# A scan on VectorE in place of matmul sums in stick breaking, and the first projection as filling work

## The chip, the cores and the metric

One core of a Trainium2 chip. The time is that of one execution on the device, in microseconds (us); lower is better. The engines are TensorE (PE: matmuls; PEld is its weight load), VectorE (DVE), ScalarE (ACT), GpSimd (POOL) and SyncE (SP, which issues DMAs). Each runs its own instruction queue in the order in which the program was written out, and waits on semaphores for the others.

## The reference

Two layers of a transformer: 512 tokens, width 1024. Each layer mixes two attentions and then runs a convolutional feed-forward part. The first attention (sparse, 8 heads) gives `o_nsa`; the second is stick breaking:

```python
z = jnp.einsum('bqhd,bkhd->bhqk', q[:, q0:q1], k[:, :q1]) * scale
log_1m = jnp.where(strict, -jax.nn.softplus(z), 0.0)
later = lax.cumsum(log_1m, axis=3, reverse=True) - log_1m
w = jnp.where(strict, jnp.exp(jax.nn.log_sigmoid(z) + later), 0.0)
...
y = g_a * (o_nsa @ w_proj_nsa) + g_b * (o_sb @ w_proj_sb)
return y @ w_out
```

`strict` keeps the keys before the query. Since log_sigmoid(z) is z - softplus(z), the weight of a key is exp(z minus the sum of softplus over this key and all later ones before the query). `g_a` and `g_b` are sigmoids of two more projections of the input.

## The kernel before

Activations lie transposed, with features on partitions and the 512 tokens along the row. All matmuls run in fp32r; a number is split in a high part (a cast on ScalarE, line 105 for weights) and a low part (a subtraction, line 106), and a product takes three matmuls (high x high, low x high, high x low). A full tile over 1024 features is 24 matmuls of 512 columns, a projection tile over 512 features is 12.

The text below calls the stage from the first score matmul of stick breaking to the first matmul of the output projection (`bk<-yh`) "the stage". In it PE has two kinds of work. The first is the eight heads (`Head`). For a head, `scores` writes 1280 columns of PSUM (`Z`, two buffers): keys on partitions, queries along the row, four blocks of 512, 384, 256 and 128 columns. `soft1` to `soft4` build softplus from |z| with Exp and Ln on ScalarE, take max(z, 0) to it on VectorE (line 1066), clear the diagonal blocks on GpSimd (`diag_keep`, line 1034) and split it (lines 1071, 1072). `sums` adds the suffix sums into the same PSUM by matmuls against two constant matrices, `negl` (a triangle of -1) and `nones` (all -1): 10 matmuls for the high part, 10 for the low. `weights1` and `weights2` take Exp, clear the diagonal again and split (lines 1089, 1090); `out` multiplies with the values into `pv`, and the result is added to `o_s`.

The second kind is filling work, tiles that write the one PSUM bank `f`: queries and keys of head pairs 2 and 3 (`sb_pair`; each evacuated by line 781) and the eight tiles of the second gate `gb` (`gate`, line 802). After them comes the projection of the first attention's output `o_n` with gate `ga` (`projection(ga, ...)`, eight tiles in six banks `bk`, evacuated by line 1147), then that of `o_s` with `gb`.

The sparse attention ends just ahead of the stage: transposes `tp` are copied by ScalarE into `pt` and multiplied into `pv`; in between PE puts the values' tiles (`sb_values`).

The order on each engine is not written by hand: a scheduler writes it out at build time from priorities and its own idea of durations. `tc.high_priority(offset=2000)` lifts heads 4 to 7 over the filling tiles. At run time nothing is reordered, so an instruction waits behind everything ahead of it in its queue.

Of the kernel before, what the change touches and what calls it, by code (L numbers as in the profile page):

```python
# [158 lines left out]
def run_kernel(ctx, tc, xT, pos, inv, vec, pew, cw1, w_m, w_vn, w_pr, w_o, w_u, w_d, xmid, rot, out):  # L159
# [116 lines left out]
    negl = cp.tile([128, 128], FR, name="negl")  # L276
# [7 lines left out]
    def constants():  # L284
        with pool("scr") as sp:
            scr = sp.tile([128, 128], F, name="scr")
            scr2 = sp.tile([128, 2, 128], F, name="scr2")
            nc.gpsimd.memset(ident, 1.0)
            nc.gpsimd.affine_select(out=ident, in_=ident, compare_op=OP.is_equal, fill=0.0, base=0,
                                    pattern=[[-1, 128]], channel_multiplier=1)  # L290

            nc.gpsimd.memset(scr, -1.0)
            nc.gpsimd.affine_select(out=scr, in_=scr, compare_op=OP.is_ge, fill=0.0, base=0,
                                    pattern=[[-1, 128]], channel_multiplier=1)
# [12 lines left out]
            nc.vector.tensor_copy(identb, ident)  # L307
            nc.vector.tensor_copy(negl, scr)
            nc.vector.tensor_copy(cbias, scr2)

    def rope_tables(rt, res, wait):
# [212 lines left out]
    for l in range(DEPTH):  # L524
# [8 lines left out]
        def slot(k, name, dt=F):  # L533
            return rp.tile([128, SLOT], dt, name=nm(name), tag=k)
# [291 lines left out]

        def split_o(src, c0, c1):

            hi, lo = slot(c0, "oh", FR), slot(c1, "ol", FR)
            s2 = src.rearrange("p k t -> p (k t)")  # L830
            for k in range(4):
# [188 lines left out]

        with temps(3) as sw, pool("pz", space=PSUM) as pz:

            c0 = [0, 512, 1024, 896]
            wd = [512, 384, 256, 128]

            def blk(t, j, q0=0):

                o = c0[j] + (max(q0, j) - j) * 128
                return t[:, o:c0[j] + wd[j]]

            def diag_keep(t):
                for j in range(4):
                    d = t[:, c0[j]:c0[j] + 128]
                    nc.gpsimd.affine_select(out=d, in_=d, compare_op=OP.is_gt, fill=0.0, base=0,  # L1034
                                            pattern=[[1, 128]], channel_multiplier=-1)

            class Head:
                def __init__(self, h):
# [5 lines left out]
                def scores(self):  # L1044
# [4 lines left out]
                    ks = lambda j: slice(j * 128, j * 128 + 128)  # L1049

                    for j in range(4):
                        mm(blk(Z, j), kk[:, e, ks(j)], qh[:, e, j * 128:], j != 3, False)
                    for j in range(4):
                        mm(blk(Z, j), kk[rr, e, ks(j)], qlo[rr, j * 128:], False, True)

                def soft1(self):
                    t = self.t = self.tile("sbt", "sbt")
                    nc.scalar.activation(t, self.Z[:, :1280], AF.Abs)  # L1058
# [5 lines left out]
                def soft3(self):  # L1064
                    t = self.t
                    nc.vector.scalar_tensor_tensor(t, self.Z[:, :1280], 0.0, t, op0=OP.max, op1=OP.add)
                    diag_keep(t)

                def soft4(self):
                    self.hi, self.lo = self.tile("sph", "sph", FR), self.tile("spl", "spl", FR)  # L1070
                    nc.vector.tensor_copy(self.hi, self.t)
                    nc.vector.tensor_sub(self.lo, self.t, self.hi.bitcast(F))

                def sums(self):
                    Z = self.Z
                    for part in (self.hi, self.lo):
                        for j in range(4):
# [4 lines left out]
                def weights1(self):  # L1082
                    w_ = self.w = self.tile("sbw", "sbw")
                    act(w_, self.Z[:, :1280], AF.Exp)

                def weights2(self):
                    diag_keep(self.w)
# [15 lines left out]
            def run_heads(hs):  # L1103
                for h in hs:
# [253 lines left out]
```

## Time and profile before

| what | value |
|---|---|
| median of three runs | 1656.79 us (1656.38 to 1658.58) |
| the profiled execution, its own time | 1653.88 us |
| its span, first to last instruction | 1652.2 us |
| PE, VectorE, ScalarE, GpSimd busy | 97%, 68%, 50%, 13% |
| mean granted clock of PE | 0.989 of full |

Busy shares are over the whole span; where an engine waits is seen in the lists of waits and in the timeline, which gives each instruction's start, length and the idle time before it with the instruction that ended it.

### The profile page before, as it was taken

How to read it: one execution, taken by the hardware profiler on the slowest of the kernel's cores; microseconds unless marked ns; L12 is line 12 of the kernel's file. 1: busy time of each engine (PE TensorE's matmuls, PEld its weight loads, DVE VectorE, ACT ScalarE, POOL GpSimd, SP SyncE). 2: the span in 40 equal slices, each digit the busy share in tenths (PEclk: the TensorE clock that was granted, in tenths of full speed). 3: DMA queues.
4: the chain of work that ended last, by engine and by line, in shares of the span. 5: the costliest groups of instructions: out<-in, count | busy, mean ns of one | idle time of the engine just before them, and what ended most of it. 6: DMA issues, size and time to landing. Idle time of an engine off the chain costs nothing.

```text
span 1652.2 us, 23212 instructions
## 1 busy us (share of the span) xinstructions
PE 1609.0 (97%) x8970; PEld 1393.2 (84%) x8970; DVE 1118.2 (68%) x1659; ACT 825.3 (50%) x1338; POOL 211.1 (13%) x252
## 2 busy tenths in 40 slices
PE   9899999999999999999999999999999999999997
PEld 9878887888998888888998788878889988888896
DVE  8775676767578777733677666677676687776235
ACT  6555565654555444423555455575536454444233
POOL 0034442120000000000000453322200000000000
PEclk9989999999999999999999999999999999999999
DMA  6521112114412233333664211112153132322344
GB/s 228 152 77 52 39 39 64 52 64 141 132 61 88 91 102 91 97 93 107 195 204 129 71 44 47 39 64 64 52 180 114 39 99 93 102 91 95 98 128 141
DMA packets 53501, 159.42 MB, mean 96 GB/s; under 512 B 6544, under 2 KB 12176, under 8 KB 53392
## 3 DMA queue, kind: packets, MB, share of 16 engines
q1 hardware_dynamic: 51088, 152.00, 29.0%
q0 software_dynamic: 1296, 4.72, 0.8%
q8 instruction: 70, 1.15, 0.3%
q10 hardware_dynamic: 1008, 1.23, 0.3%
q14 instruction: 39, 0.32, 0.1%
HBM read 144.30 MB, written 4.72 MB: 90 GB/s over the span
## 4 chain that ended last, share of the span: by engine, by line
PE 82%; DVE 8%; ACT 5%; issue 2%; DMA 2%; POOL 1%; SPq 1%; ACTq 0%; DVEq 0%; POOLq 0%
PE bk L382 56%; PE f L382 15%; PE pv L382 3%; PE Z L382 3%; PE S L382 2%; PE tp L935 2%; POOL sbt L1034 1%; DVE wlo L106 1%; DVE st L906 1%; DMA rs<-rf 1%; DMA x<-in_xT 1%; ACT whi L105 0%; ACT sbt L226 0%; ACT sbt L1058 0%; ACT sbw L226 0%
## 5 line engine op out<-in xcount | busy, mean ns | idle before, releaser
L105 ACT CAST whi<-wraw 128x1024 fp32r<-128x1024 f32 (+2 forms) x235 | 241.2, 1027 | 342.7 <-PE bk L382 254.3
L106 DVE TENSOR_TENSOR wlo<-wraw,whi 128x1024 fp32r<-128x1024 f32 (+2 forms) x209 | 248.8, 1191 | 184.1 <-ACT whi L105 181.4
L382 PE MATMUL bk<-h_hi,whi 128*128 128x512 f32 (+1 forms) x768 | 286.5, 374 | 2.1 <-ACT f_t L1260 1.7
L382 PE MATMUL bk<-h_hi,wlo 128*128 128x512 f32 (+1 forms) x768 | 286.4, 374 | 0.0
L382 PE MATMUL bk<-h_lo,whi 128*128 128x512 f32 (+1 forms) x768 | 286.2, 373 | 0.0
L382 PE MATMUL f<-h_hi,whi 128*128 128x512 f32 x448 | 184.4, 412 | 11.7 <-DVE gate L802 9.2
L382 PE MATMUL f<-h_lo,whi 128*128 128x512 f32 x448 | 179.1, 400 | 0.0
L382 PE MATMUL f<-h_hi,wlo 128*128 128x512 f32 x448 | 178.6, 399 | 0.0
L382 PEld LDWEIGHTS bk<-h_hi,whi 128*128 128x128 f32 x768 | 145.6, 190 | 27.7 <-ACT f_t L1260 1.9
L382 PEld LDWEIGHTS bk<-h_hi,wlo 128*128 128x128 f32 x768 | 145.5, 190 | 25.4 <-DVE wlo L106 0.4
L382 PEld LDWEIGHTS bk<-h_lo,whi 128*128 128x128 f32 x768 | 145.6, 190 | 24.8
L382 PE MATMUL bk<-ah,wlo 128*128 128x256 f32 (+1 forms) x484 | 161.7, 334 | 2.4 <-DVE wlo L106 2.4
L382 PE MATMUL bk<-ah,whi 128*128 128x256 f32 (+1 forms) x484 | 160.4, 331 | 0.0
L382 PE MATMUL bk<-al,whi 128*128 128x256 f32 (+1 forms) x484 | 160.2, 331 | 0.0
L382 PEld LDWEIGHTS f<-h_hi,whi 128*128 128x128 f32 x448 | 86.4, 193 | 30.6 <-DVE gate L802 10.0
L382 PEld LDWEIGHTS bk<-ah,wlo 128*128 128x128 f32 x484 | 91.8, 190 | 12.5 <-DVE wlo L106 3.4
L1228 DVE TENSOR_TENSOR cu<-bk,r 128x512 f32<-128x512 f32 x88 | 60.2, 687 | 61.2 <-PE bk L382 60.9
L382 PEld LDWEIGHTS f<-h_hi,wlo 128*128 128x128 f32 x448 | 85.9, 192 | 18.5
L382 PEld LDWEIGHTS f<-h_lo,whi 128*128 128x128 f32 x448 | 86.5, 193 | 15.5
L382 PEld LDWEIGHTS bk<-ah,whi 128*128 128x128 f32 x484 | 91.9, 190 | 8.7
L382 PEld LDWEIGHTS bk<-al,whi 128*128 128x128 f32 x484 | 91.9, 190 | 8.7
L382 PE MATMUL bk<-h_hi,wh 128*128 128x256 f32 x512 | 96.0, 285 | 0.0
(241 smaller groups left out, 3174.3 us busy)
## 6 DMA issues: line engine op xcount, KB each, us to landing
wraw<-in_w_u SPq DMA_DIRECT2D x88, 512.0 KB, 3.5
wraw<-in_w_m SPq DMA_DIRECT2D x72, 512.0 KB, 3.3
wraw<-in_w_d SPq DMA_DIRECT2D x44, 512.0 KB, 3.5
wraw<-in_w_d SPq DMA_DIRECT2D x22, 384.0 KB, 3.1
wraw<-in_w_pr SPq DMA_DIRECT2D x16, 512.0 KB, 3.6
wraw<-in_w_o SPq DMA_DIRECT2D x16, 512.0 KB, 3.5
rs<-rf SPq DMA_DIRECT2D x56, 64.0 KB, 2.8
wraw<-in_cw SPq DMA_DIRECT2D x4, 512.0 KB, 4.6
```

What stands on the lines that cost most here:

```text
L105: self.nc.scalar.copy(hi[:, c], raw[:, c])
L106: eng.tensor_sub(lo[:, c], raw[:, c], hi.bitcast(F)[:, c])
L382: last_mm[0] = nc.tensor.matmul(o, a, b, start=first, stop=last, skip_group_check=True)
L906: nc.vector.tensor_reduce(self.st[:, 0:2], self.S[:, :self.n].rearrange("p (j b k) -> p b j k", j=self.i + 1, b=2), axis=AX.XY, op=OP.max, ...
L935: nc.tensor.transpose(tp[:, b * 128:(b + 1) * 128], self.P[:, (c + b) * 128:(c + b + 1) * 128], ident)
L1034: nc.gpsimd.affine_select(out=d, in_=d, compare_op=OP.is_gt, fill=0.0, base=0, pattern=[[1, 128]], channel_multiplier=-1)
L1228: nc.vector.tensor_mul(u, b, r2)
```

## The change

Stick breaking now has queries on partitions and keys along the row, so that the suffix sum runs along a row. `scores` adds a bias block `sbias` (0 below the diagonal, -1e30 from it on) with four bf16 matmuls. `soft1` also takes Relu(z) into `r`; `sums` is a reversed `tensor_tensor_scan` on VectorE in four pieces (512, 384, 256 and 128 columns; line 1075) that adds both parts of softplus up, and a subtraction from `Z` (line 1077). The weights are then transposed on PE, ten 128 x 128 blocks a head in fp32 (line 1085), into the PSUM of `Z`, and split from there: high part on ScalarE (line 1088, `wh`), low part on VectorE (line 1089). GpSimd's masks and the 20 matmuls of sums go. `Z` stays in use until line 1089.

The projection of `o_n` moves ahead of heads 4 to 7 in program order and writes the bank `f`; its low part goes to the buffer of `h_lo`. The two sigmoids of `ga` move ahead of heads 0 to 3.

```diff
+                    for i in (3, 2, 1, 0):
+                        mm(rows(Z, i), qh[:, e, qt(i)], kk[:, e, :(i + 1) * 128], i != 0, False)
+                    for i in (3, 2, 1, 0):
+                        mm(rows(Z, i)[:, i * 128:], identb, sbias, False, False)
+                    for i in (3, 2, 1, 0):
+                        mm(rows(Z, i), qlo[rr, qt(i)], kk[rr, e, :(i + 1) * 128], False, True)
...
+                    r = self.r = self.tile("sbr", "sbr", bufs=2)
+                    nc.scalar.activation(r, z, AF.Relu)
...
-                def sums(self):
-                    Z = self.Z
-                    for part in (self.hi, self.lo):
-                        for j in range(4):
-                            mm(blk(Z, j), negl, blk(part, j), False, False)
-                            for j2 in range(j + 1, 4):
-                                mm(blk(Z, j, j2), nones, blk(part, j2), False, part is self.lo and j2 == 3)
...
+                def sums(self):
+
+                    t, r = self.t, self.r
+                    for i in (3, 2, 1, 0):
+                        nc.vector.tensor_tensor_scan(rows(r, i, True), rows(t, i, True), rows(r, i, True), 0.0,
+                                                     op0=OP.add, op1=OP.add)
+                    nc.vector.tensor_sub(t, self.Z[:, :1280], r)
+
+                def weights(self):
                     t = self.t
...
+                    act(t, t, AF.Exp)
+                    wT = self.Z
+                    for j in range(4):
+                        for i in range(j, 4):
+                            nc.tensor.transpose(blk(wT, j)[:, (i - j) * 128:(i - j + 1) * 128],
+                                                rows(t, i)[:, j * 128:(j + 1) * 128], ident)
                     self.whi, self.wlo = self.tile("wh", "wh", FR), self.tile("wl", "wl", FR)
...
+                    nc.scalar.copy(self.whi, wT[:, :1280])
+                    nc.vector.tensor_sub(self.wlo, wT[:, :1280], self.whi.bitcast(F))
...
+            for i in range(2):
+                act(ga[i], ga[i], AF.Sigmoid)
             run_heads(range(4))
...
             gate(gb, 0, "k1")
             gate(gb, 1, "sa")
+
+            n_hi, n_lo = split_o(o_n, "sb", None)
+            for m in range(8):
+                if m % 2 == 0:
+                    wt = W.get()
+                b = fbank("f")
+                drain(gemm(b, wt, n_hi, n_lo, range(4), woff=4 * (m % 2), ahead=2 if m % 2 else 1))
+                with tc.high_priority():
+                    nc.vector.tensor_mul(at(ga, m), b, at(ga, m))
             with tc.high_priority(offset=2000):
                 run_heads(range(4, 8))
...
-                for m in projection(ga, n_hi, n_lo):
-                    pass
```

How the written order changes is shown at three places of the first layer. The first is ScalarE's queue at the end of the sparse attention: `P_315` is the last softmax, `gate_340` and `gate_345` are `ga`, `pt` the copies of transposed weights. Before:

```order
L226 ACTIVATE P_315_2090,st_314_2083<-S_309_2046,st_314_2083 128x4x128 x2
L968 COPY pvl_311_2069<-pv_310_2052 64x256
L944 CAST pt_303_2030<-tp_312_2073 128x4x128
L944 CAST pt_305_2032<-tp_313_2078 128x4x128
L105 CAST whi30_2747<-wraw30_2631 128x1024
```

And of the change:

```order
L226 ACTIVATE P_315_2092,st_314_2085<-S_309_2048,st_314_2085 128x4x128 x2
L233 ACT_TABLE_LOAD
L226 ACTIVATE gate_340_2344<-gate_340_2344 128x2048
L226 ACTIVATE gate_345_2473<-gate_345_2473 128x2048
L233 ACT_TABLE_LOAD
L969 COPY pvl_311_2071<-pv_310_2054 64x256
L945 CAST pt_303_2032<-tp_312_2075 128x4x128
L945 CAST pt_305_2034<-tp_313_2080 128x4x128
L105 CAST whi30_2749<-wraw30_2633 128x1024
```

Two table loads and both sigmoids of `ga` now stand ahead of the copies of `tp_312` and `tp_313`.

The second is PE's queue where head 0 (`Z_367`) comes back after its scores; `f_407` before and `f_403` now are filling tiles. Before:

```order
L382 MATMUL f_407_3068<-h_hi_99,wlo30_2748 128x512
L382 MATMUL Z_367_2771<-sph_369_2789,negl_94 128x512
L382 MATMUL Z_367_2771<-sph_369_2789,nones_93 128x384
L382 MATMUL Z_367_2771<-sph_369_2789,nones_93 128x256
L382 MATMUL Z_367_2771<-sph_369_2789,nones_93 128x128
L382 MATMUL Z_367_2771<-sph_369_2789,negl_94 128x384
```

And of the change:

```order
L382 MATMUL f_403_3061<-h_hi_99,whi31_3008 128x512
L382 MATMUL f_403_3061<-h_lo_100,whi31_3008 128x512
L382 MATMUL f_403_3061<-h_hi_99,wlo31_3009 128x512
L1085 MATMUL Z_367_2776<-ident_91,sbt_368_2789 128x128 x10
L382 MATMUL f_405_3100<-h_hi_99,whi32_3047 128x512
```

Where the sums of the first half stood, the ten transposes of the finished weights stand now; ahead of them come two filling tiles, behind them `f_405`.

The third is VectorE's queue for heads 0 and 1 (`sbt_368` and `sbr_369`, then `sbt_377` before, `sbt_375` and `sbr_376` now); `sbz` is the evacuation of a filling tile. Before:

```order
L1066 SCALAR_TENSOR_TENSOR sbt_368_2780<-Z_367_2771,sbt_368_2780 128x1280
L789 TENSOR_TENSOR qlo_404_3028<-sbz_406_3060,sbst_403_3027 64x512 x2
L1071 CAST sph_369_2789<-sbt_368_2780 128x1280
L781 SCALAR_TENSOR_TENSOR sbz_408_3099<-f_407_3068,r2_90 128x512
L1072 TENSOR_TENSOR spl_370_2790<-sbt_368_2780,sph_369_2789 128x1280
L106 TENSOR_TENSOR wlo32_3094<-wraw32_2711,whi32_3093 128x1024
```

And of the change (the scan appears under its opcode's name, SCALAR_TENSOR_TENSOR, at line 1075):

```order
L1075 SCALAR_TENSOR_TENSOR sbr_369_2793<-sbt_368_2789,sbr_369_2793 128x512
L1075 SCALAR_TENSOR_TENSOR sbr_369_2793<-sbt_368_2789,sbr_369_2793 128x384
L1075 SCALAR_TENSOR_TENSOR sbr_369_2793<-sbt_368_2789,sbr_369_2793 128x256
L1075 SCALAR_TENSOR_TENSOR sbr_369_2793<-sbt_368_2789,sbr_369_2793 128x128
L789 TENSOR_TENSOR sbst_395_2981<-sbz_400_3053,sbst_395_2981 64x512 x2
L1077 TENSOR_TENSOR sbt_368_2789<-Z_367_2776,sbr_369_2793 128x1280
L1075 SCALAR_TENSOR_TENSOR sbr_376_2844<-sbt_375_2841,sbr_376_2844 128x512
L1075 SCALAR_TENSOR_TENSOR sbr_376_2844<-sbt_375_2841,sbr_376_2844 128x384
L1075 SCALAR_TENSOR_TENSOR sbr_376_2844<-sbt_375_2841,sbr_376_2844 128x256
L1075 SCALAR_TENSOR_TENSOR sbr_376_2844<-sbt_375_2841,sbr_376_2844 128x128
L781 SCALAR_TENSOR_TENSOR sbz_404_3092<-f_403_3061,r2_90 128x512
```

The evacuation of `f_403`, which `f_405` needs, stands behind the whole scan of head 1.

## Rows read from the trace of the kernel before

**Rows 1.** The page, part 1: busy time of each engine.

```profile
PE 1609.0 (97%) x8970; PEld 1393.2 (84%) x8970; DVE 1118.2 (68%) x1659; ACT 825.3 (50%) x1338; POOL 211.1 (13%) x252
```

**Rows 2.** PE's waits, 258 to 400 us: total, times, longest (us).

```profile
PE f L382 <- DVE sbz L781: 0.8, 1, 0.8
PE Z L382 <- ACT sbw L226: 0.6, 1, 0.6
PE pv L382 <- DVE wl L1090: 0.3, 1, 0.3
PE Z L382 <- DVE sph L1071: 0.2, 1, 0.2
PE bk L382 <- ACT whi L105: 0.2, 1, 0.2
```

**Rows 3.** Timeline of PE: first score matmul, and first of the output projection.

```profile
258.33 0.80 PE L382 MATMUL Z<-sbst 128*128 128x512 f32 x4
...
411.66 0.40 PE L382 MATMUL bk<-yh,whi 128*128 128x512 f32 x1
```

**Rows 4.** Timeline of PE: a filling tile, a half of head 0's sums, what follows.

```profile
270.56 0.45 PE L382 MATMUL f<-h_hi,whi 128*128 128x512 f32 x1
...
275.43 0.39 PE L382 MATMUL Z<-spl,negl 128*128 128x512 f32 x1
...
276.74 0.45 PE L382 MATMUL f<-h_hi,whi 128*128 128x512 f32 x1
```

**Rows 5.** Timeline of PE, sparse attention: a bf16 bias matmul, six transposes.

```profile
221.90 0.28 PE L382 MATMUL S<-cbias,identb 128*128 128x256 bf16 x1
222.02 0.84 PE L935 MATMUL tp<-ident,P 128*128 128x128 f32 x6
```

**Rows 6.** Groups by line and shape: busy us, mean ns of one, idle before.

```profile
L105 ACT CAST whi<-wraw 128x1024 fp32r<-128x1024 f32 x211 | 221.7, 1051 | 294.9 <-PE bk L382 206.6 <-PE f L382 52.7 <-issue 30.7
...
L226 ACT ACTIVATE sbt<-sbt 128x1280 f32<-128x1280 f32 x32 | 40.8, 1274 | 0.7
...
L1066 DVE SCALAR_TENSOR_TENSOR sbt<-Z,sbt 128x1280 f32<-128x1280 f32 x16 | 23.8, 1489 | 8.5 <-ACT sbt L226 8.5
...
L1058 ACT ACTIVATE sbt<-Z 128x1280 f32<-128x1280 f32 x16 | 19.9, 1243 | 23.3 <-DVE spl L1072 20.0 <-PE Z L382 3.3
...
L906 DVE TENSOR_REDUCE st<-S 128x2 f32<-128x1024 f32 x16 | 19.5, 1216 | 3.2 <-PE S L382 3.2
...
L1071 DVE CAST sph<-sbt 128x1280 fp32r<-128x1280 f32 x16 | 13.7, 855 | 7.8 <-POOL sbt L1034 5.3 <-PE f L382 2.4
...
L906 DVE TENSOR_REDUCE st<-S 128x2 f32<-128x256 f32 x16 | 6.3, 415 | 1.0 <-PE S L382 1.0
```

**Rows 7.** Timeline of PE: last matmul of a filling tile, first of the next.

```profile
261.98 0.39 PE L382 MATMUL f<-h_hi,wlo 128*128 128x512 f32 x1
263.15 0.50 PE L382 MATMUL f<-h_hi,whi 128*128 128x512 f32 x1 [0.78 <-DVE sbz L781]
```

**Rows 8.** Timeline, ScalarE and PE: the sparse attention's end, and the sigmoids.

```profile
241.44 0.37 ACT L968 COPY pvl<-pv 64x256 f32<-64x256 f32 x1
...
244.95 0.59 ACT L944 CAST pt<-tp 128x512 fp32r<-128x512 f32 x1 [3.14 <-PE tp L935]
...
246.35 0.28 PE L382 MATMUL pv<-pt,vN 128*128 128x256 f32 x1
...
367.32 1.28 ACT L233 ACT_TABLE_LOAD   x1
368.62 7.33 ACT L226 ACTIVATE gate<-gate 128x2048 f32<-128x2048 f32 x4
```

**Rows 9.** Windows: length, busy of each engine, granted clock, DMA share, GB/s.

```profile
116.00:120.00 4.00, 0.17 (x2) 0.00 (x0) 3.75 (x4) 1.08 (x2) 3.10 (x2) 0.80 0.00 0
120.00:124.00 4.00, 3.81 (x9) 3.04 (x10) 2.29 (x7) 1.02 (x4) 1.04 (x1) 0.50 0.37 131
124.00:128.00 4.00, 4.00 (x16) 3.20 (x16) 0.00 (x0) 0.00 (x0) 0.00 (x0) 0.85 0.00 0
```

More of the change, by code (lines that the diff above doesn't have):

```diff
@@ L275, in run_kernel @@
     nones = cp.tile([128, 128], FR, name="nones")
-    negl = cp.tile([128, 128], FR, name="negl")
+    sbias = cp.tile([128, 128], BF, name="sbias")
     cbias = cp.tile([128, 2, 128], BF, name="cbias")
@@ L290, in constants @@
                                     pattern=[[-1, 128]], channel_multiplier=1)
-            nc.gpsimd.memset(scr, -1.0)
-            nc.gpsimd.affine_select(out=scr, in_=scr, compare_op=OP.is_ge, fill=0.0, base=0,
+            nc.gpsimd.memset(scr, 0.0)
+            nc.gpsimd.affine_select(out=scr, in_=scr, compare_op=OP.is_gt, fill=NEG, base=0,
                                     pattern=[[-1, 128]], channel_multiplier=1)
@@ L307, in constants @@
             nc.vector.tensor_copy(identb, ident)
-            nc.vector.tensor_copy(negl, scr)
+            nc.vector.tensor_copy(sbias, scr)
             nc.vector.tensor_copy(cbias, scr2)
@@ L827, in split_o @@
         def split_o(src, c0, c1):
-            hi, lo = slot(c0, "oh", FR), slot(c1, "ol", FR)
             s2 = src.rearrange("p k t -> p (k t)")
+            hi = slot(c0, "oh", FR)
+            lo = slot(c1, "ol", FR) if c1 else h_lo.rearrange("p k t -> p (k t)")
             for k in range(4):
@@ L1021, in run_kernel, with rows, blk @@
         with temps(3) as sw, pool("pz", space=PSUM) as pz:
-            c0 = [0, 512, 1024, 896]
             wd = [512, 384, 256, 128]
[L1026 to L1031, printed above, removed]
-                for j in range(4):
-                    d = t[:, c0[j]:c0[j] + 128]
-                    nc.gpsimd.affine_select(out=d, in_=d, compare_op=OP.is_gt, fill=0.0, base=0,
-                                            pattern=[[1, 128]], channel_multiplier=-1)
+            cq = [896, 1024, 512, 0]
+            ck = [0, 512, 1024, 896]
+            def rows(t, i, rev=False):
+                s_ = t[:, cq[i]:cq[i] + wd[3 - i]]
+                return s_[:, ::-1] if rev else s_
+            def blk(t, j):
+                return t[:, ck[j]:ck[j] + wd[j]]
             class Head:
@@ L1048, in scores @@
                     rr = slice(e * 64, e * 64 + 64)
[L1049 to L1054, printed above, removed]
+                    qt = lambda i: slice(i * 128, i * 128 + 128)
+                    for i in (3, 2, 1, 0):
+                        mm(rows(Z, i), qh[:, e, qt(i)], kk[:, e, :(i + 1) * 128], i != 0, False)
@@ L1056, in soft1 @@
+                    for i in (3, 2, 1, 0):
+                        mm(rows(Z, i)[:, i * 128:], identb, sbias, False, False)
+                    for i in (3, 2, 1, 0):
+                        mm(rows(Z, i), qlo[rr, qt(i)], kk[rr, e, :(i + 1) * 128], False, True)
                 def soft1(self):
-                    t = self.t = self.tile("sbt", "sbt")
-                    nc.scalar.activation(t, self.Z[:, :1280], AF.Abs)
+                    t = self.t = self.tile("sbt", "sbt", bufs=2)
+                    z = self.Z[:, :1280]
@@ L1059, in soft1 @@
+                    nc.scalar.activation(t, z, AF.Abs)
                     act(t, t, AF.Exp, scale=-1.0)
+                    r = self.r = self.tile("sbr", "sbr", bufs=2)
+                    nc.scalar.activation(r, z, AF.Relu)
                 def soft2(self):
                     act(self.t, self.t, AF.Ln, bias=1.0)
-                def soft3(self):
-                    t = self.t
-                    nc.vector.scalar_tensor_tensor(t, self.Z[:, :1280], 0.0, t, op0=OP.max, op1=OP.add)
-                    diag_keep(t)
@@ L1069, in soft4 @@
[L1069 to L1072, printed above, removed]
-                def sums(self):
-                    Z = self.Z
-                    for part in (self.hi, self.lo):
-                        for j in range(4):
-                            mm(blk(Z, j), negl, blk(part, j), False, False)
-                            for j2 in range(j + 1, 4):
-                                mm(blk(Z, j, j2), nones, blk(part, j2), False, part is self.lo and j2 == 3)
@@ L1082, in weights1 @@
[L1082 to L1087, printed above, removed]
+                def sums(self):
[4 more added lines that the diff above has]
+                    nc.vector.tensor_sub(t, self.Z[:, :1280], r)
@@ L1090, in weights2 @@
-                    nc.vector.tensor_sub(self.wlo, self.w, self.whi.bitcast(F))
+                    nc.scalar.copy(self.whi, wT[:, :1280])
+                    nc.vector.tensor_sub(self.wlo, wT[:, :1280], self.whi.bitcast(F))
                 def out(self):
@@ L1130, in run_kernel @@
             m_last = []
-            n_hi, n_lo = split_o(o_n, "sb", "vn")
             s_hi, s_lo = split_o(o_s, "q0", "k0")
-            for g_ in (ga, gb):
-                for i in range(2):
-                    act(g_[i], g_[i], AF.Sigmoid)
+            for i in range(2):
+                act(gb[i], gb[i], AF.Sigmoid)
             with pool("py", space=PSUM) as py:
```

6 lines of the change are left out of this document (1 added, 5 removed).

## The prediction

> **What bounds the kernel now.** First the page: TensorE (PE) is busy 97% of the span [rows 1], and its mean clock is 0.989 of full (the table above). So a microsecond of matmul work is worth about a microsecond wherever PE does not wait, and a wait costs as much. The list of waits over the first layer's stick breaking (258 to 400 us) shows what PE waits for there: five waits, 2.1 us in all [rows 2]. The other engines keep up because PE's queue always has a filling matmul ready. Whatever the change does, it shows on PE, as less work or as more waiting. I measure a layer from the first score matmul of head 0 to the first matmul of the output projection: 258.33 to 411.66, or 153.3 us [rows 3].
>
> I call the heads h0 to h7 and the filling tiles K2, Q3, K3 (`sb_pair`), G0 to G7 (`gate`) and P0 to P7 (first attention's projection).
>
> **PE work removed and added.** One half of a head's sums (10 matmuls) takes 275.43 to 276.74, 1.31 us [rows 4]; two halves, eight heads: 21.0 us per layer gone. Added are ten fp32 transposes a head. Six in a row take 0.84 us with the last one's own 0.27 in it, so 0.114 each [rows 5]: 1.14 a head, 9.1 per layer. Also added are four bf16 bias matmuls of 128 columns. The 256-column one is followed 0.12 us later by the next instruction [rows 5], so 0.06 each; with their weight loads I take 0.3 a head, 2.4 per layer. Scores, outputs and the eight P tiles keep their matmuls. Net: 21.0 - 9.1 - 2.4 = **9.5 us per layer less PE work.** GpSimd loses its masks and gives nothing back, since PE never waited for it there [rows 2].
>
> **What a head now costs the other engines.** Prices are from [rows 6]. ScalarE: Abs 1.24, Exp 1.27, Ln 1.27 and last Exp stay (the last now from SBUF, 1.27); Relu and the copy `wh` are new and are priced like the Abs, which reads the same 1280 columns of PSUM: 1.24 each. VectorE loses a max-add, two casts and two subtractions (1.49 + 0.86 + 1.49 + 0.86 + 1.49; the subtractions have the max-add's shape) and gets the scan and two subtractions.
>
> The trace holds no scan. Reductions of 256 and 1024 columns take 0.415 and 1.216 us: 1.04 ns a column and 0.15 fixed. Below, then: four pieces, 1280 columns, one pass: 1.9 us. Above: two separate passes, 3.9. Each element needs two adds, and the second must be finished before the next element's first can start; I take two passes with the fixed part paid once, 2 x 1.33 + 4 x 0.15 = 3.3. In a queue a VectorE row starts about 0.08 before the one ahead ends, so the walk below uses 3.1 (and 1.7 and 3.6 for the bounds).
>
> The rows show only one-pass operations at 1.04 ns a column. [...]
>
> So VectorE's total hardly moves (6.2 before, 6.3 now), but ScalarE carries 2.5 us more, and the chain of one head is longer: score, Abs, (Relu), Exp, Ln, scan, subtraction, Exp, before its transposes.
>
> **The walk.** I follow the written order of the engines, from PE's first score matmul of h0 = 0. The 21 filling matmuls from 270.56 to 275.43 take 0.232 each [rows 4], so a full tile (24) 5.5 and a P tile (12) 2.8; scores, two passes of 0.8 [rows 3] and the bias, 1.95. The bank `f` is one buffer: when two filling tiles stand next to each other, PE waits for the evacuation, 0.94 us from the last start to the next [rows 7]; with VectorE free I charge 1.0.
>
> - h0's and h1's scores end at 1.95 and 3.9. ScalarE does Abs and Relu of both (2.2 to 7.3), both Exps (to 9.9), a weight cast (10.9), Ln of h0 at 12.2. The scan runs 12.25 to 15.35, then two `L789` pieces (16.6), the subtraction (18.1), Exp (19.4).
> - PE: K2 to 9.45, wait 1.0, Q3 to 16.0. Now it needs h0's transposes: **wait 3.5**, to 19.5. They end at 20.5, and K3 needs Q3's evacuation, which stands on VectorE behind h1's scan (18.1 to 21.2) and ends at 21.85: **wait 1.4**.
> - h2, h3: G1 waits 0.5 (evacuation behind h2's scan), G2 1.0, G3 1.5 (behind h3's scan and subtraction), G4 1.0.
> - h5: Ln at 82.1, scan 85.25, cast, subtraction 87.8, Exp 89.15; PE is at its transposes at 87.1: **2.1**.
> - P0 0.45, P1 1.05 (bank again; before, the projection had six banks).
> - h7: Ln 109, scan 113, `wlo` 114.1, subtraction 115.5, Exp 116.8; PE is there at 112.95: **3.95**.
> - The two sigmoids of `gb` with their table loads come before h7's `wh` on ScalarE (to 123.2); P4 1.0, h7's output 0.55, P5 1.4, P6 1.0.
>
> Together **21.5 us of waiting** where 2.1 were [rows 2]; the output projection starts at 159.6. The same walk with the scan at 1.7 gives 13.5 and 151.6: 5.9 us per layer for each us of scan.
>
> **Ahead of it.** The `ga` sigmoids now stand on ScalarE before `pvl_311` and the copies of `tp_312`, which ran at 241.44 and 244.95. Two table loads of 1.28 and two sigmoids of 1.9 are 6.3 us [rows 8]; from 241.4 that ends at 247.7, and the copies at 249.2. The output matmul that needs them ran at 246.35 [rows 8]. PE has 0.4 us of `sb_values` transposes to put in: a wait of 2.4, and 0.4 more at the last output, **2.8 per layer**. In exchange these loads leave the projection's start, where they cost PE nothing that the waits show [rows 2].
>
> **Sum.** Terms per layer: -9.5 - 2.1 + 21.5 + 2.8 = +12.7. The walk's end gives 159.6 + 2.8 - 153.3 = +9.1: it charges PE nothing for small switches, which fill some of the waits. I take the middle, +11. Layer 1 is written in nearly the same order. 1653.9 + 22 = **1676 us**. That is on the profiled execution's own 1653.88 (span 1652.2 and 1.7 around it), 2.9 below the median of the three runs. Bounds of the scan: below, (4.7 + 1.1) / 2 = +3 per layer, 1660; above, +14, 1682.
>
> **Rivals.**
> - *The scan runs at one pass.* For it: every VectorE row of the trace does. Against: none of those feeds a result into the next element. 1660.
> [...]
> - *Faster: the PE work comes through.* VectorE and ScalarE have half of their time free over the stage; if their queues catch up before PE comes to the transposes, the waits stay at 2.1 and the sigmoids are covered: 1653.9 - 19 = 1635. It decides when waits and sigmoids together stay below 11.6 us per layer. Against: the walk finds more than that even with the one-pass scan, because h0 and h1 start together and nothing is ready behind Q3.
>
> **How the numbers follow.** Chances: forecast 0.58, clock 0.12, one-pass scan 0.11, faster 0.19. The first three hold 1655 to 1694; the low end goes to 1652 for a walk that is too strict, and the 1635 case stays outside. The forecast's own range is 1666 to 1686. A measurement of this kernel tells about 0.2% (3.3 us) from no change. Faster 0.19, same 0.07 (part of the one-pass case), slower 0.74.
>
> **What would show it.** Right: scan pieces of 1.22, 0.95, 0.69 and 0.42 us (512 to 128 columns); PE idle in front of h0's transposes for VectorE or ScalarE, 3 us or more; waits of filling tiles `f` for `sbz` and `gate` over 1 us; a wait for ScalarE's `pt` just ahead of h0; the stage from first score to output projection near 164 us. Wrong: scan pieces half as long, the sums' 21 us gone and PE's waits there still near 2 us. The prediction falls if the list of PE's waits over the stage holds under 11 us.

## The result, and the profile after

The changed kernel takes 1671.95 us (median of 4 runs, 1671.29 to 1672.67), the kernel before 1656.59 beside it (4 runs, 1655.81 to 1658.58): a ratio of 1.0097, interval 1.0085 to 1.011. It is 15 us slower, on the side that was forecast. The forecast, 1676, is 22 above the 1653.88 that it was counted from; that is one execution, 2.7 below the median beside the change. The profiled execution took 1671.29, its span 1669.4 us: 17.2 more than the span before.

TensorE's row on the page after, beside [rows 1]:

```profile
PE 1593.3 (95%) x8874; PEld 1371.8 (82%) x8874; DVE 1113.6 (67%) x1675; ACT 865.6 (52%) x1374; POOL 155.0 (9%) x124
```

PE lost 15.7 us of work, as a saving should show, and the span grew all the same. So PE's idle time grew by 32.9. Where, the timeline says: the first score matmul and the first matmul of the output projection, both layers, beside [rows 3].

```profile
262.20 0.80 PE L382 MATMUL Z<-sbst 128*128 128x512 f32 x4
...
419.78 0.40 PE L382 MATMUL bk<-yh,whi 128*128 128x512 f32 x1
...
1085.87 0.80 PE L382 MATMUL Z<-sbst 128*128 128x512 f32 x4
...
1244.90 0.40 PE L382 MATMUL bk<-yh,whi 128*128 128x512 f32 x1
```

Before, layer 1 had these two at 1073.73 and 1227.02. So layer 0's stage starts 3.9 late and takes 157.6 instead of 153.3, and layer 1's, 4.0 more late, takes 159.0 instead of 153.3. The rest of the program gives 0.7 back. 3.9 + 4.2 + 4.0 + 5.7 - 0.7 = 17.2: that is all of it.

What happens inside a stage is read from a view of windows, whose columns are length, busy time of PE, its weight loads, VectorE, ScalarE and GpSimd, then granted clock, DMA share and GB/s. First the two stages before, then after:

```profile
258.33:411.66 153.33, 151.07 (x750) 125.93 (x749) 112.33 (x125) 86.42 (x88) 30.33 (x68) 1.00 0.25 83
1073.73:1227.02 153.29, 151.00 (x749) 125.95 (x749) 112.31 (x125) 86.41 (x88) 30.18 (x68) 1.00 0.25 83
```

```profile
262.20:419.78 157.58, 142.05 (x699) 115.00 (x699) 108.39 (x132) 99.54 (x101) 2.30 (x4) 0.99 0.24 81
1085.87:1244.90 159.03, 144.07 (x698) 117.05 (x698) 108.47 (x132) 99.39 (x101) 2.15 (x4) 0.97 0.24 80
```

PE idles 15.5 and 15.0 us of a stage (length less busy) where it idled 2.3. And the granted clock, 1.00 before, is 0.99 and 0.97. PE's waits in layer 0's stage, with total, times and longest, beside [rows 2]:

```profile
PE Z L1085 <- ACT sbt L226: 7.2, 3, 3.4
PE f L382 <- DVE gate L1127: 2.9, 4, 0.9
PE f L382 <- ACT pvl L1098: 0.9, 1, 0.9
PE f L382 <- ACT whi L105: 0.9, 1, 0.9
PE f L382 <- DVE gate L802: 0.9, 1, 0.9
PE f L382 <- ACT wh L1088: 0.9, 1, 0.9
PE f L382 <- DVE sbz L781: 0.8, 1, 0.8
PE pv L382 <- DVE o_s L1100: 0.8, 1, 0.8
```

Two kinds. Three times PE stands in front of a head's transposes (h0 2.85, h5 0.99, h7 3.38) until ScalarE's last Exp has ended: the chain of a head is late. Nine times the one bank `f` changes hands between two filling tiles, and PE waits for its evacuation, mostly 0.8 to 0.95. Where the list names ScalarE, VectorE's evacuation had ended only 0.07 to 0.12 earlier (at 272.39, 317.27 and 327.91), so it is the same gap. The scan's pieces, with mean ns of one:

```profile
L1075 DVE TENSOR_TENSOR_SCAN sbr<-sbt,sbr 128x512 f32<-128x512 f32 x8 | 9.8, 1220 | 4.5 <-ACT sbt L226 4.4
L1075 DVE TENSOR_TENSOR_SCAN sbr<-sbt,sbr 128x384 f32<-128x384 f32 x8 | 7.5, 932 | 0.0
...
L1075 DVE TENSOR_TENSOR_SCAN sbr<-sbt,sbr 128x256 f32<-128x256 f32 x8 | 5.3, 665 | 0.0
...
L1075 DVE TENSOR_TENSOR_SCAN sbr<-sbt,sbr 128x128 f32<-128x128 f32 x8 | 3.2, 398 | 0.0
```

Ahead of the stage stand `ga`'s sigmoids, beside [rows 8], first on ScalarE and then what PE waited for there:

```profile
242.31 1.28 ACT L233 ACT_TABLE_LOAD   x1
243.61 3.72 ACT L226 ACTIVATE gate<-gate 128x2048 f32<-128x2048 f32 x2
247.34 1.28 ACT L233 ACT_TABLE_LOAD   x1
248.64 0.37 ACT L969 COPY pvl<-pv 64x256 f32<-64x256 f32 x1
```

```profile
248.15 0.66 PE L820 MATMUL f<-ident,sbz 128*128 128x128 f32 x4 [0.78 <-DVE sbz L817]
249.77 0.35 PE L382 MATMUL pv<-pt,vN 128*128 128x256 f32 x1 [0.96 <-DVE o_n L971]
250.49 0.63 PE L936 MATMUL tp<-ident,P 128*128 128x128 f32 x4 [0.37 <-DVE pt L947]
```

The copies `pvl` and `pt` stand behind 6.3 us of ScalarE, and PE waits 2.1 us there, where it waited 0.3 before. PE is 0.9 late here already: a tile of `sb_values` well ahead of the sigmoids starts at 225.82 instead of 224.94.

The clock is the third thing. In windows of 4 us behind three of the long waits it fell, to 0.50 of full at the lowest, in layer 0 behind h0, in layer 1 behind h0 and h7:

```profile
280.00:284.00 4.00, 2.23 (x12) 1.87 (x13) 4.00 (x6) 1.79 (x3) 0.00 (x0) 0.89 0.00 0
284.00:288.00 4.00, 4.00 (x14) 3.13 (x13) 3.94 (x5) 2.82 (x3) 0.00 (x0) 0.68 0.63 197
1104.00:1108.00 4.00, 2.56 (x13) 2.13 (x14) 4.00 (x7) 1.77 (x3) 0.00 (x0) 0.72 0.00 0
1108.00:1112.00 4.00, 4.00 (x10) 3.07 (x10) 3.94 (x4) 2.50 (x2) 0.00 (x0) 0.50 0.63 197
1112.00:1116.00 4.00, 4.00 (x21) 3.28 (x20) 0.55 (x2) 0.67 (x1) 0.00 (x0) 0.93 0.00 0
1200.00:1204.00 4.00, 2.14 (x11) 2.14 (x11) 2.50 (x3) 3.44 (x3) 0.00 (x0) 0.67 0.40 131
1204.00:1208.00 4.00, 4.00 (x21) 3.25 (x19) 0.00 (x0) 3.98 (x3) 0.00 (x0) 0.91 0.00 0
```

The share of clock that is missing, times 4 us, is an estimate of what a fall costs: 1.7, 3.4 and 1.7 us. h7's wait is 3.38 in both layers. In layer 0 no fall follows it, and ten transposes take 1.31; in layer 1 they take 2.40. So the length of a wait alone does not decide it.

### The profile page after: what moved, and what is told of

Read it like the earlier page. It is cut to its first block, busy times and chain, and to the rows that moved or that the text cites. A ratio compares the mean times of both kernels' runs of the same rounds, so it can differ in the third digit from the quotient of the medians.

```text
span 1669.4 us, 22875 instructions
## 1 busy us (share of the span) xinstructions
PE 1593.3 (95%) x8874; PEld 1371.8 (82%) x8874; DVE 1113.6 (67%) x1675; ACT 865.6 (52%) x1374; POOL 155.0 (9%) x124
## 4 chain that ended last, share of the span: by engine, by line
PE 77%; DVE 11%; ACT 7%; issue 3%; DMA 1%; SPq 1%; ACTq 0%; DVEq 0%
PE bk L382 54%; PE f L382 15%; PE pv L382 3%; PE S L382 2%; DVE sbr L1075 2%; PE tp L936 2%; ACT sbt L226 1%; DVE wlo L106 1%; PE Z L382 1%; DMA rs<-rf 1%; DVE st L907 1%; ACT sbt L1063 1%; SPq L619 1%; PE Z L1085 1%; DVE sbt L1077 1%
## 5 line engine op out<-in xcount | busy, mean ns | idle before, releaser
L382 PE MATMUL f<-h_lo,whi 128*128 128x512 f32 x512 | 205.9, 402 | 0.0
L382 PE MATMUL f<-h_hi,whi 128*128 128x512 f32 x448 | 186.0, 415 | 19.1 <-DVE gate L802 10.3
L382 PEld LDWEIGHTS f<-h_lo,whi 128*128 128x128 f32 x512 | 99.5, 194 | 17.9
```

The costliest lines, as they stand in the source:

```text
L382: last_mm[0] = nc.tensor.matmul(o, a, b, start=first, stop=last, skip_group_check=True)
```

## The experiments

Twelve kernels ran. All stand beside the kernel before on the same chip; "stage" is the length in layers 0 and 1, PE's busy time in it and its clock, read as above.

| run | median, us | ratio to before | stage, us | PE busy | clock |
|---|---|---|---|---|---|
| the change | 1671.95 | 1.0085 to 1.011 | 157.6, 159.0 | 142.1, 144.1 | 0.99, 0.97 |
| e1 scan alone | 1691.88 | 1.02 to 1.0227 | 171.4, 170.7 | 148.0, 148.3 | 0.93, 0.93 |
| e2 projection alone | 1674.1 | 1.0093 to 1.012 | 157.7, 159.2 | 151.3, 151.7 | 1.00, 1.00 |
| e3 late `ga` | 1667.84 | 1.0057 to 1.0083 | 159.5, 159.2 | 144.7, 144.8 | 0.97, 0.97 |
| e4 addition for scan | 1660.55 | 1.0006 to 1.0024 | 151.1, 150.6 | 139.9, 139.6 | 1.00, 1.00 |
| e5 h0 first | 1665.98 | 1.0027 to 1.0063 | 156.1, 156.1 | 144.6, 144.6 | 0.97, 0.97 |
| e7 h0 first, late `ga` | 1668.12 | 1.006 to 1.0084 | 159.5, 158.9 | 146.2, 145.3 | 0.96, 0.97 |
| e8 projection alone, late `ga` | 1671.6 | 1.0077 to 1.0103 | 160.0, 160.0 | 152.4, 152.4 | 1.00, 1.00 |
| e9 `wlo` on GpSimd | 1687.75 | 1.017 to 1.0206 | 165.4, 165.6 | 145.6, 145.6 | 0.96, 0.96 |
| e10 the same, h0 first | 1689.41 | 1.0184 to 1.0236 | 166.8, 166.8 | 145.4, 145.5 | 0.96, 0.96 |
| e11 the same, late `ga` | 1686.76 | 1.0162 to 1.0202 | 169.3, 169.3 | 147.3, 147.5 | 0.94, 0.94 |
| e15 h0 first, `wl` of h2 first | 1663.4 | 1.0022 to 1.0044 | 154.4, 154.4 | 143.3, 143.3 | 0.98, 0.98 |
| e16 the same, late `ga` | 1662.99 | 1.0023 to 1.0048 | 156.5, 156.9 | 142.8, 142.8 | 0.99, 0.99 |

**The two halves of the change apart.** e1 keeps the scan and takes the projection back to the end of the stage, with `ga`'s sigmoids beside `gb`'s as they were:

```diff
-            for i in range(2):
-                act(ga[i], ga[i], AF.Sigmoid)
             run_heads(range(4))
...
-            n_hi, n_lo = split_o(o_n, "sb", None)
-            for m in range(8):
...
+            n_hi, n_lo = split_o(o_n, "sb", "vn")
...
+                for m in projection(ga, n_hi, n_lo):
+                    pass
```

> The scan alone: the projection of o_n is back behind the heads, in six banks, with the four sigmoids where they were. Theory of the walk (PE waits for the longer chain of a head, and for the one bank f): h0, h5 and the waits of G1 to G4 stay as after (8 us of a layer), the early sigmoids cost nothing (-3.9 a layer), the waits of the P tiles go (-4), but without P tiles h6 and h7 stand back to back and PE waits for their chains, 6 us or more; 1662 to 1670. Rival, the moved projection is the loss: 1655 or less, and PE's wait in front of h7's transposes stays at 3.4 or falls.

1691.88: 35 above the kernel before, and 22 above even the top of the walk's range. The order of things was the walk's, not the rival's; the size was not. The end of layer 0's stage in PE's timeline:

```profile
365.11 2.39 PE L1085 MATMUL Z<-ident,sbt 128*128 128x128 f32 x10 [4.77 <-ACT sbt L226]
...
368.81 0.79 PE L382 MATMUL pv<-wh,vS 128*128 128x512 f32 x1 [1.31 <-ACT wh L1088]
...
372.69 2.40 PE L1085 MATMUL Z<-ident,sbt 128*128 128x128 f32 x10 [3.08 <-ACT sbt L226]
...
385.37 0.79 PE L382 MATMUL bk<-oh,whi 128*128 128x512 f32 x1 [5.40 <-DVE wl L1089]
```

Without P tiles h6 and h7 have nothing beside them: 14.6 us of waits in 25. The granted clock is 0.50 from 364 to 376 us, and ten transposes take 2.4 instead of 1.3. The stage idles 23 us.

e2 is the kernel before with the projection and `ga`'s sigmoids moved; the matmul sums stay:

```diff
+            for i in range(2):
+                act(ga[i], ga[i], AF.Sigmoid)
             run_heads(range(4))
...
+            n_hi, n_lo = split_o(o_n, "sb", None)
+            for m in range(8):
...
-            n_hi, n_lo = split_o(o_n, "sb", "vn")
...
-                for m in projection(ga, n_hi, n_lo):
-                    pass
```

> The projection move alone: the sums stay as matmuls with their split and masks, the projection of o_n is filling work in bank f, and ga's sigmoids stand ahead of the last pt copies. Theory of the walk: nothing is saved on PE, the sigmoids cost 2 to 4 a layer ahead of h0 and the P tiles wait up to 0.9 each for the bank; 1664 to 1672. Rival, the scan's chain is the whole loss: within 3 of the kernel before.

1674.1, just past the range and well away from the rival: 17 above before. PE's work in the stage is that of before (151.3 against 151.1), but it idles 6.4 and 7.6 us, P tiles waiting up to 1.6 and 1.8 for the bank. h0 starts at 262.18, 3.85 late, as in the change, and in layer 1 5.7 late. So 35 for the scan alone, 17 for the move alone, and 15 for both: **the move is worth 20 us once the scan is there, and costs 17 where it is not.** The two prices do not add up to the sum. e3 below has late sigmoids like e1 and is 24 us faster, so the gain is that of the P tiles among the heads; the early sigmoids take 4 of it.

**The early sigmoids.** e3 moves two lines:

```diff
-            for i in range(2):
-                act(ga[i], ga[i], AF.Sigmoid)
             run_heads(range(4))
...
+            for i in range(2):
+                act(ga[i], ga[i], AF.Sigmoid)
             n_hi, n_lo = split_o(o_n, "sb", None)
```

> The changed kernel with ga's two sigmoids moved behind the last gate tile, in front of the split of o_n. Theory of the walk: the waits ahead of h0 (3.9 a layer in the profile: 262.20 against 258.33) go; the two table loads and sigmoids (6.3 us of ScalarE) come back in part as a longer wait for h6 or h7, up to 3 a layer; 1664 to 1669. Rival, the later start of h0 has another cause: 1670 to 1673.

1667.84, within the range. h0's scores start 3.1 us earlier in layer 0 (259.12) and 3.0 in layer 1, so most of their delay was the sigmoids'; 1.9 of it comes back in layer 0's stage and 0.1 in layer 1's. PE no longer waits at h0's transposes; in their place Q3 waits for K2's evacuation, which now stands on VectorE behind h0's scan:

```profile
274.05 0.77 PE L382 MATMUL f<-h_hi,whi 128*128 128x512 f32 x1 [3.90 <-DVE sbz L781]
```

e8 makes the same edit on e2:

> The projection move alone (sums as matmuls), with ga's sigmoids behind the last gate tile. The move with early sigmoids was measured at 1674.1, 17 above the kernel before; its profile has h0 3.85 later in layer 0 and 5.7 in layer 1, and P tiles that wait up to 1.6 for the bank. Theory: the two are separate prices and the later sigmoids give back 3 to 4 a layer, 1666 to 1668, so the bank's waits are the larger part that stays. Rival, the sigmoids come back as waits of the heads: 1672 or more.

1671.6: between the two and near the rival. It is 2.5 less than e2, but the intervals of the two ratios overlap, so that gain is not certain. h0's scores start at 260.29, 1.9 earlier, and layer 0's stage takes 2.3 more. So in layer 0 what the late sigmoids give back ahead of h0 is lost again in the stage.

**The scan's price.** e4 leaves the suffix sums out: a plain addition of the same pieces, from front to back where the scan runs from back to front.

```diff
-                        nc.vector.tensor_tensor_scan(rows(r, i, True), rows(t, i, True), rows(r, i, True), 0.0,
-                                                     op0=OP.add, op1=OP.add)
+                        nc.vector.tensor_add(rows(r, i), rows(t, i), rows(r, i))
```

> The changed kernel with a plain addition of the same pieces in place of the scan, so the suffix sums are left out; its pieces should take 1.2 ns a column less, about 1.4 us less a head. Theory of the walk (5.9 us of a layer for each us of scan): 8 less a layer, but no more than the waits at h0, h5, h7 and what follows them hold: 5 to 8 a layer, 1656 to 1662. Rival, ScalarE's queue and not the scan makes the transposes late: less than 3 in all, 1669 to 1672.

1660.55, within the theory's range; 0.06% to 0.24% above the kernel before, so still no gain. Its pieces:

```profile
L1075 DVE TENSOR_TENSOR sbr<-sbt,sbr 128x512 f32<-128x512 f32 x8 | 5.5, 688 | 4.5 <-ACT sbt L226 4.4
...
L1075 DVE TENSOR_TENSOR sbr<-sbt,sbr 128x128 f32<-128x128 f32 x8 | 2.3, 284 | 0.0
```

A column costs (688 - 284) / 384 = 1.05 ns in the addition and (1220 - 398) / 384 = 2.14 in the scan, with 0.15 and 0.12 us fixed; no run tells the two directions apart. Four pieces take 1.70 instead of 2.97. The shorter piece takes 4.1 us of PE's idle time out of a stage (15.2 to 11.1), and all of its falls of the clock:

```profile
262.79:413.92 151.13, 139.87 (x699) 113.85 (x698) 98.54 (x132) 99.48 (x101) 2.30 (x4) 1.00 0.27 84
1082.12:1232.72 150.60, 139.61 (x698) 113.75 (x698) 98.65 (x132) 99.31 (x101) 2.15 (x4) 1.00 0.27 84
```

PE's program is nearly that of the change, so this run also shows its work without a fall of the clock: 139.7, which is 11.3 less than before. Both stages are shorter than before (153.3), and still the kernel is not faster, because h0's scores start 4.5 late in layer 0 and 6.1 more in layer 1.

**ScalarE's order at h0.** e5 puts h0's (and h4's) whole chain ahead of the next head's; for that it moves Relu behind Ln, in every head:

```diff
+                    op = nc.scalar.activation(t, z, AF.Abs)
+                    if self.h % 4 == 1:
+                        after(op, relus[-1])
                     act(t, t, AF.Exp, scale=-1.0)
-                    r = self.r = self.tile("sbr", "sbr", bufs=2)
-                    nc.scalar.activation(r, z, AF.Relu)
...
                     act(self.t, self.t, AF.Ln, bias=1.0)
+                    ln = table["users"][-1]
+                    r = self.r = self.tile("sbr", "sbr", bufs=2)
+                    op = nc.scalar.activation(r, self.Z[:, :1280], AF.Relu)
+                    after(op, ln)
+                    relus.append(op)
```

> The changed kernel with ScalarE's order at h0 and h4 alone altered: Abs, Exp, Ln and Relu of h0 come ahead of the Abs of h1 (in the profile after, Abs and Relu of both heads come first and Ln of h0 starts 8.2 us after its Abs). h0's scan should start 3 to 4 us earlier. Theory of the walk: the wait of 2.85 in front of h0's transposes and the 0.85 behind it go, with them the fall of the clock there, and h1 is not late, since K3 covers it: 3 to 4 a layer, 1664 to 1667. Rival, the wait only moves to h1 or to the bank f (K2's evacuation waits behind h0's scan on VectorE): within 2 of after, 1670 to 1673.

The median, 1665.98, is in the theory's range, and PE no longer waits at h0's transposes. But the wait for K2's evacuation has grown from 0.88 to 1.74, as the rival had it, and the ten executions lie between 1656.2 and 1670.5, nearly in the order of their clocks (0.991 to 0.983). The profiled one (1668.69) shows where a clock goes:

```profile
315.16 1.14 PE L382 MATMUL Z<-sbst 128*128 128x512 f32 x4 [2.18 <-DVE wl L1096]
```

```profile
312.00:316.00 4.00, 1.82 (x9) 1.27 (x7) 4.00 (x5) 2.32 (x2) 0.00 (x0) 0.94 0.40 131
316.00:320.00 4.00, 4.00 (x18) 3.39 (x18) 0.83 (x1) 1.24 (x1) 0.00 (x0) 0.50 0.44 135
```

A new wait: the scores of h4 need the bank of h2, which VectorE's `wl` subtraction of h2 still reads, and that stands behind h3's scan and subtraction. e7 joins e5 and e3:

> Both: h0's chain first on ScalarE, and ga's sigmoids behind the last gate tile. With the sigmoids late alone 1667.8 was measured, of which 3.9 a layer is one wait for K2's evacuation behind h0's scan. If the terms add: 1667.8 less 2 x 3 to 4 = 1660 to 1662. Rival, the evacuation still stands behind a scan (now an earlier one): 1665 or more.

1668.12, the rival's case. PE's timeline shows why:

```profile
274.73 0.77 PE L382 MATMUL f<-h_hi,whi 128*128 128x512 f32 x1 [4.42 <-DVE sbz L781]
```

Q3 waits for K2's evacuation, and that stands on VectorE behind h0's scan. An earlier scan is only earlier in the way.

e15 mends the wait at h4 by one dependency, e16 adds the late sigmoids:

```diff
-                    nc.vector.tensor_sub(t, self.Z[:, :1280], r)
+                    op = nc.vector.tensor_sub(t, self.Z[:, :1280], r)
+                    if self.h == 3:
+                        after(op, lows[2])
...
-                    nc.vector.tensor_sub(self.wlo, wT[:, :1280], self.whi.bitcast(F))
+                    lows[self.h] = nc.vector.tensor_sub(self.wlo, wT[:, :1280], self.whi.bitcast(F))
```

> h0's chain first on ScalarE, and on VectorE the wl subtraction of h2 ahead of the subtraction of h3. With the first edit alone the executions lay between 1656 (clock 0.991) and 1670 (0.983), and its profile shows a wait of 2.18 for that wl ahead of h4's scores (315.16 and 1137.76), each followed by 8 us at the half clock or near it. Theory (the clock falls behind a wait of this length, and the fall is what is lost): the wait shrinks to about 0.8, the falls there go, and all executions come to the fast end, 1650 to 1658. Rival (the falls have another cause): the spread stays, median 1662 or more.

> The same with ga's sigmoids behind the last gate tile. h0's scores should start some 3 us earlier in each layer; with h0's chain first this gave nothing back (1668.1), since a wait of 4.4 to 4.8 for K2's evacuation stood behind h0's scan and the clock fell behind it. Theory: that wait and its fall stay, 1655 to 1664, above the run without late sigmoids. Rival: the terms add, 2 to 6 below it.

1663.4 and 1662.99. The wait at h4 is 0.8 as expected and no fall follows it. But two other waits have a fall behind them, and the first of these is short, with one of 0.38 ahead of it at 323.85:

```profile
325.61 0.76 PE L382 MATMUL f<-h_hi,whi 128*128 128x512 f32 x1 [1.27 <-DVE gate L802]
...
372.70 0.50 PE L382 MATMUL f<-oh,whi 128*128 128x512 f32 x1 [2.84 <-DVE gate L1136]
```

```profile
324.00:328.00 4.00, 2.73 (x7) 1.94 (x8) 4.00 (x6) 0.74 (x1) 0.00 (x0) 0.71 0.00 0
372.00:376.00 4.00, 3.30 (x9) 2.65 (x10) 3.18 (x4) 0.79 (x1) 0.00 (x0) 0.68 0.27 63
```

The second is P1's wait for P0's evacuation. The spread has shrunk (1659.8 to 1663.7), yet to the wrong end; the expected 1650 to 1658 is missed, and the median is the rival's. In e16 the wait for K2's evacuation stays, as expected (4.4). Its stages take 2.1 and 2.5 longer than e15's and start 3.4 and 2.0 earlier, so it ends level with e15 and not above it. These two are the fastest found that leave nothing out: 9 us under the change, and still 0.2% to 0.5% above the kernel before.

**VectorE relieved by GpSimd.** e9 sends sixteen `wlo` halves of each layer to GpSimd, which the scan has left idle:

```diff
         for i in list(range(12, 16)) + list(range(24, 32)):
-            it(w_m[l, i])
+            it(w_m[l, i], eng=nc.gpsimd)
         for i in range(8):
-            it(w_pr[l, i])
+            it(w_pr[l, i], eng=nc.gpsimd if i < 4 else nc.vector)
```

> The changed kernel with the low halves of the weights of the stage (L106, 12 fills of w_m and the four of the moved projection) made on GpSimd, which has 2.3 us of work in a stage of 157. On VectorE they cost 1.2 us each (23.1 us for 19 in layer 0's stage) and some stand between a head's scan and its subtraction (345.93, 362.30 and 372.97 in the profile after); on GpSimd the same shape took 2.4 us. Theory (VectorE's queue, scan with all that stands around it, makes the heads late): the waits at h5, h7 and of some bank handoffs shrink by about 1 us each, 2 to 4 a layer, and a fall of the clock at h7 goes with them; 1661 to 1667. Rival (ScalarE and the bank f set the waits, VectorE has room): 1670 to 1673; a third, GpSimd's longer halves come too late for the fills: over 1675.

1687.75. That is in the third case by its number and not by its reason: no wait of PE in the stage ended with a GpSimd instruction. VectorE ran 14 instructions fewer in layer 0's stage, about 17 us, and was still busy 107.4 instead of 108.4. Several of its instructions with both operands in SBUF had grown, the scan's pieces of 512 and 256 columns (1220 and 665 ns in the change) and others (`h_lo<-o_n,oh` took 676):

```profile
L1075 DVE TENSOR_TENSOR_SCAN sbr<-sbt,sbr 128x512 f32<-128x512 f32 x8 | 12.7, 1584 | 9.8 <-ACT sbt L226 9.7
...
L1077 DVE TENSOR_TENSOR sbt<-Z,sbr 128x1280 f32<-128x1280 f32 x8 | 11.8, 1478 | 0.0
L1075 DVE TENSOR_TENSOR_SCAN sbr<-sbt,sbr 128x256 f32<-128x256 f32 x8 | 11.7, 1467 | 0.0
...
L835 DVE TENSOR_TENSOR h_lo<-o_n,oh 128x512 fp32r<-128x512 f32 x4 | 4.7, 1222 | 0.0
```

One scan in VectorE's timeline, its third piece by itself, and GpSimd's instruction at the same time:

```profile
304.78 5.09 DVE L1075 TENSOR_TENSOR_SCAN sbr<-sbt,sbr 128x512 f32<-128x512 f32 x4 [2.29 <-ACT sbt L226]
...
306.77 2.79 DVE L1075 TENSOR_TENSOR_SCAN sbr<-sbt,sbr 128x256 f32<-128x256 f32 x1
```

```profile
306.55 2.46 POOL L106 TENSOR_TENSOR wlo<-wraw,whi 128x1024 fp32r<-128x1024 f32 x1 [7.45 <-PE pv L382]
```

Four pieces take 5.09 instead of 2.97, and all of it is in the third, which starts 0.22 behind GpSimd's instruction, takes 2.79 instead of 0.67 and ends 0.55 behind it. GpSimd's took 2.46, near the 2.43 of the change. The piece grew by 2.12, and GpSimd's still ran for 2.24 of it; that the piece stood still until then is the author's reading, since the timeline gives starts and lengths alone. The subtraction `sbt<-Z,sbr`, which reads PSUM and one operand from SBUF, kept its 1.48. The order of the queues changed with the edit too, so not every microsecond of the 16 comes from these longer instructions. e10 and e11 have the same halves on GpSimd; their VectorE ran as many instructions in layer 0's stage as e9's (118, where the change has 132) and was busy 111.6 and 109.5 us:

> Low halves on GpSimd and h0's (h4's) chain first on ScalarE. The latter alone ran from 1656 to 1670 with the clock between 0.991 and 0.983, and one of its waits (2.2 us, scores of h3 behind the wl subtraction on VectorE) lay ahead of a fall of the clock. Theory: with 19 us less on VectorE that wait goes and the falls with it; 1648 to 1656. Rival, the wait stays: 1660 or more.

> Low halves on GpSimd and ga's sigmoids behind the last gate tile. Late sigmoids alone: 1667.8, with a wait of 3.9 us for K2's evacuation behind h0's scan. Theory: that wait stays (no low half stands ahead of it), the rest as in the run with GpSimd alone, so that run's time less 4. Rival: nothing on top of 1667.8, 1666 or more.

1689.41 is far over what was expected; 1686.76 is 1.0 under e9, where 4 was expected. Over both layers e10's waits in front of transposes come to 26.5 us (12 of them), e11's to 23.6 (8), where the change has 14.4 (6).

## Why the prediction was right, and where its terms were off

The mechanism held: PE loses work, gains more waiting, and the waiting is that of late heads, of the one bank `f`, and of the sigmoids ahead of h0. Per layer, forecast against measured:

- **PE work: -9.5 forecast, -11.3 measured** (139.7 in e4 against 151.0). Counted from each start to the next with idle time left out, as the forecast counted, the sums took 21.8 in layer 0 where 21.0 stood, e4's transposes 8.1 instead of 9.1, its bias 2.6 instead of 2.4, and its scores 0.6 less than before. The term was too small by 1.8.
- **Scan: 3.3, in a queue 3.1, forecast; 2.97 measured.** The four pieces came at 1.22, 0.93, 0.67 and 0.40, where 1.22, 0.95, 0.69 and 0.42 stood. The price of two passes with one fixed part, an assumption between the bounds, came out: 2.14 ns a column in the scan against 1.05 in e4's addition. Not every row ahead of the prediction is at 1.04 ns a column: the cast in [rows 6] takes 855 ns for 1280 columns, 0.67 each.
- **Waits in the stage: 21.5 forecast, 15.2 measured; 19.4 more than before against 13.0.** This is the term that was mis-sized. The places were right: h0 3.5 forecast and 2.85 measured, h5 2.1 and 0.99, h7 3.95 and 3.38. The bank `f` was forecast to make PE wait eleven times, 11.3 in all; in layer 0 it did nine times, 7.3 in all. Before six of these nine evacuations VectorE had been idle. K3's did stand behind h1's scan, as the walk said, and cost 0.85 instead of 1.4. Part of the difference is one of counting: the starts in [rows 7] are 1.17 apart, which is 0.94 more than the 0.23 of a filling matmul, and the list of waits gives 0.78 for the same gap, since it counts idle time alone.
- **Sigmoids: 2.8 forecast, 3.9 and 4.0 measured.** The copies stood behind the second table load as the walk said (`pvl` at 248.64, forecast 247.7). e3, which moves the sigmoids and nothing else, gives 3.1 and 3.0 back, so the price itself was near. The remaining 0.9 of layer 0 is there before the sigmoids run (225.82 against 224.94); what delays layer 1 by the last 1.0 was not followed.
- **Clock: nothing in the sum.** PE is busy 2.3 and 4.3 longer than e4's 139.7 for the same work. The 0.12 for the clock stood for falls behind h0's and h7's waits in both layers, each as large as the one in [rows 9], (0.20 + 0.50 + 0.15) x 4 = 3.4 us by the same estimate, and so for 1676 + 13.6 = 1690. The waits were the right ones, the size was twice what came: three falls instead of four, of 1.7 to 3.4 us by the windows.

Layer 0: -11.3 + 13.2 + 2.3 + 3.9 = 8.1, layer 1: -11.3 + 12.7 + 4.3 + 4.0 = 9.7; the forecast was 11. The errors partly paid for each other: waits too large by 6.4 and work saved too small by 1.8 on one side, clock too small by 3.3 and sigmoids by 1.1 on the other. The middle between 12.7 and 9.1 took another 1.7 a layer off, and the start from 1653.9 took 2.7 off the total. So 1676 against 1672 is better than its parts, by luck. Of the signs named beforehand, the scan's pieces came within 0.03. The idle time at h0 stayed just under 3 us, the waits for `f` under 1 but for one of 1.28 in layer 1, and the stage at 157.6 and 159.0 where 164 stood. The waits ahead of h0 ended with VectorE's `sbz`, `o_n` and `pt`, not with ScalarE's `pt`.

The slope of the walk held: 5.9 us of a layer for each us of scan were forecast, and e4 shows 6.5 and 8.4 us of stage, 7.4 in the mean, for 1.27 us. Its make-up did not: 4.1 are waits, the rest is the clock. Over the whole program e4 is 11.4 faster than the change, 5.7 a layer, since its stages start later. The bound worked out for a one-pass scan, 1660, is what the addition measured.

The "faster" rival was to decide where waits and sigmoids stay below 11.6 us per layer. With the saving as measured that line is 11.3 + 2.3 = 13.6. The change has 15.2 + 3.9 = 19.1, and the clock on top. e4, with its 11.1 of waits and stages that start 4.5 and 6.1 late, 5.3 in the mean, is 2.8 a layer over the line; its profiled span is 5.1 over that of before, its median 3.3, in two layers.

What stays open is what brings the clock down: behind the same wait of 3.38 it fell in one layer and not in the other, in e15 a fall stands behind waits of 0.38 and 1.27, and the executions of e5 differ by 14 us in the same program. Also open is whether a second bank for filling tiles would make the change pay; no run shows it.

## What to carry to other kernels

Where one engine is 97% busy, as here, work moved off it pays only if the chain it moves to stays ahead of that engine's queue. Add up the chain of one head over all engines, and look at what is left to cover it at the first head and at the last ones; there it showed here, with waits of 2.85 and 3.38 us. Do not price two parts of a change apart when one covers the other's holes: here 35 and 17 made 15. And a wait that is mended in one queue tends to come back in the next one, so look at the next evacuation in line before counting the gain.

## What the runs showed of the hardware

- **In e9 VectorE's instructions with two SBUF operands took longer beside GpSimd's subtractions.** Four scan pieces took 5.09 us instead of 2.97 with one GpSimd subtraction of 128x1024 (2.46 us) beside them, all of the growth in the piece of 256 columns, 2.79 instead of 0.67. Two pieces of `sbst<-sbz,sbst` at 297.41 took 2.97 instead of 1.40 with another (2.38 us, from 296.73) beside them. The subtraction `sbt<-Z,sbr`, with one operand in PSUM, kept 1.48 (1.49 at 281.84, with one from 281.70 beside it). This speaks against e9, and was not weighed before it.
- **A fall of the clock cost from half of the wait ahead of it to 1.2 times as much.** The change lost 1.7, 3.4 and 1.7 us by the windows' estimate, behind waits of 2.85, 2.85 and 3.38. Executions of one program differed by up to 14 us (e5), with mean clocks of 0.983 to 0.991; 0.008 of 1663 us is 13 us, so by this estimate the clock makes up nearly all of the difference.
